# Gate and up products of the second feed-forward part by Strassen's seven half-size products

## The chip, the cores and the metric

The kernel runs on one core of one Trainium2 chip. The number that counts is the device time of one execution in microseconds (us). A core has five engines with a queue of instructions each: PE multiplies matrices, DVE (VectorE) and ACT (ScalarE) work element by element, POOL (GpSimd) does so more slowly, and SP issues the transfers from memory. The engines meet at semaphores only, and each takes its own queue strictly in order.

## The reference

Two layers act on 512 tokens of width 1024. Each has a feed-forward part, a mixing block (three recurrences) and a second feed-forward part; a last norm ends it.

```
def swiglu(h, wg, wu, wd):
    return (jax.nn.silu(h @ wg) * (h @ wu)) @ wd

for i in range(DEPTH):
    h = rmsnorm(x, ffn1_norm[i])
    x = x + 0.5 * swiglu(h, ffn1_wg[i], ffn1_wu[i], ffn1_wd[i])
    x = x + mixing block of layer i
    h = rmsnorm(x, ffn2_norm[i])
    x = x + 0.5 * swiglu(h, ffn2_wg[i], ffn2_wu[i], ffn2_wd[i])
return rmsnorm(x, final_norm)
```

The change is in the second swiglu: `h @ wg` and `h @ wu` are 512 x 1024 times 1024 x 2816, and `@ wd` is 512 x 2816 times 2816 x 1024. All is float32.

## The kernel before, in words

Activations lie transposed: the 1024 features are eight tiles of 128 partitions by 512 tokens, `self.x`. To keep the accuracy of float32, every operand of a product is split into a high part (`whi`, `hh`) and a low part (`wlo`, `hl`), and each product is three matmuls: high by high (L263), high by low (L271), low by high (L272). `load_w` fetches a block of weights (`raw`, three buffers), takes the high part on ACT (L248) and the low part on DVE (L249).

`ffn` walks over 22 column tiles of 128. `gate` does for one of them 24 matmuls of 512 columns for the gate product and 24 for the up product, each pair in a bank of PSUM of its own (`mm`, three banks). DVE multiplies both by `rstd`, the reciprocal root of each token's mean square (L386, L387), ACT applies SiLU (L388), DVE multiplies (L389), and the result is split for the down product (L276, L277). So the norm's factor is applied behind the products, and products of a layer begin as soon as `x` times the gain is split (`norm`: L1180 on ACT, L1181 on DVE); the sum of squares is added up on POOL beside it (L346), and its small instructions come later, at the places in PE's order that `GATES` names.

The down products come in parts, `PARTS`: after four tiles (three in the last two parts), and one tile of the next part, eight products of 12 (or 9) matmuls of 512 columns add the part to `x` (L377). At the end of the second layer the last part goes by halves of the tokens, with 256 columns, and `finish` norms each half.

The order of each engine's queue comes from a scheduler that follows the order of the program, what the instructions need of each other, and when buffers come free. `run` calls `ffn` twice a layer, around `mix`.

Of the kernel before, what the change touches and what calls it, by code (L numbers as in the profile page):

```python
# [9 lines left out]
F32R = mybir.dt.float32r  # L10
# [7 lines left out]
L = 512  # L18
D = 1024
# [7 lines left out]
# tag: (elements of 4 bytes, buffers)  # L27
# [10 lines left out]
# parts of the products between the steps of the recurrence  # L38
# [20 lines left out]
# ---------------------------------------------------------------- layout of the small inputs  # L59
# [4 lines left out]
def constants():  # L64
    """masks and identities, from shapes alone"""
# [37 lines left out]
def layout(z):  # L103
    """every input, laid out by partition"""
# [64 lines left out]
# ---------------------------------------------------------------- the kernel  # L169
class Kernel:  # L170
# [63 lines left out]
    def load_w(self, src, k, m, keep=None):  # L234
        """both parts of a [128, k, m] block of weights"""
# [21 lines left out]
    def gemm(self, ps, w, act, ks=None):  # L257
# [3 lines left out]
        for k in ks or range(len(act)):  # L261
# [33 lines left out]
    def row_sums(self, parts, bank):  # L295
        """per token, the sum over partitions"""
# [8 lines left out]
    def token_rstd(self, b, n, tag):  # L305
        """(b / n + eps) ** -0.5 of each token"""
# [6 lines left out]
    def row_diag(self, b, n, tags):  # L313
        """(b / n + eps) ** -0.5 of each token, in two parts, on diagonals"""
# [13 lines left out]
    def row_wide(self, dg, out, bank):  # L328
        """the diagonal on all partitions"""
# [21 lines left out]
    def norm(self, gain, gates):  # L351
        """x * gain in two parts, and the broadcast rstd of each token"""
# [14 lines left out]
    # ------------------------------------------------------------ SwiGLU  # L367
    def ffn(self, gain, f, i, end=False):
# [27 lines left out]
        for n, (k0, nk) in enumerate(PARTS):  # L396
            # the next part's first tile goes before this part's products
# [7 lines left out]
            if end and first is None:  # L405
                # the last products by halves of the tokens, to begin the last norm early
# [16 lines left out]
    # ------------------------------------------------------------ the mixing block  # L423
    def mix(self, i):
# [16 lines left out]
        def proj(j, post):  # L441
            """projection j in steps, and what is done with it"""
# [27 lines left out]
        def add():  # L470
            # the norm of the SSD part comes last
# [53 lines left out]
        def stream():  # L525
# [5 lines left out]
            # capital: all of it, else a part  # L531
# [18 lines left out]
        def weave(main, filler, ratio, pin=True):  # L550
            """main, and the filler's steps between its own"""
# [19 lines left out]
        # the recurrence first; the other products are held back to go beside it  # L571
# [47 lines left out]
    # ------------------------------------------------------------ RWKV-7  # L619
# [11 lines left out]
    def shifted(self, ps, j, out):  # L631
        """token shift of projection tile j"""
# [8 lines left out]
    def sigmoid(self, t):  # L641
        """from tanh(x / 2)"""
        self.nc.gpsimd.tensor_scalar(out=t, in0=t, scalar1=0.5, scalar2=0.5, op0=MUL, op1=ADD)

    def rwkv_l(self, ps):
        """decay, in-context rate and gate"""
# [6 lines left out]
        # [hi, lo] beside both parts of the weights, in one product where the rows allow it  # L653
# [24 lines left out]
        for ct in range(2):  # L678
# [14 lines left out]
            # cumulative sum inside chunks of 32  # L693
# [71 lines left out]
    def to_tok(self, src, out):  # L765
        """src(ct) [128 (head, d), L] -> out [128 tok, 4 token tiles, 4 heads, 64]"""
# [10 lines left out]
    def rwkv_core(self):  # L777
        """everything that the state does not enter; J = (token tile, head), in two halves of the tokens"""
# [16 lines left out]
        # masked products inside chunks of 32  # L795
        for q, M in ((0, MB), (1, MK)):
            for h in range(2):
# [11 lines left out]
                if q == 0:  # L809
                    # minus the transposed inverse of I + A, by doubling the size of its blocks  # L810
# [58 lines left out]
    def rwkv_ends(self):  # L869
        """what a chunk does to the state, S -> P S + G, the state before each chunk, and the output"""  # L870
# [14 lines left out]
        def PG(h):  # L885
            # the state before the first chunk is zero, the one after the last is not asked for
# [32 lines left out]
        def YQ(h):  # L919
            """how the state is read, and what the chunk gives by itself"""  # L920
# [75 lines left out]
        # capital: all of it, else one step  # L996
# [26 lines left out]
        # softplus(x) = max(x, 0) + log1p(exp(-|x|)), log1p(e) = 2 atanh(e / (2 + e))  # L1023
# [30 lines left out]
    def ssd_conv(self, ps, g, j):  # L1054
        """causal convolution and SiLU of x (two tiles), B and C of a group"""
# [17 lines left out]
    def ssd_chunk(self, g, c, banks=("ms",) * 4):  # L1073
# [18 lines left out]
        # decay between the tokens of a chunk, transposed  # L1092
# [84 lines left out]
    def split_scaled(self, x, scale):  # L1177
        """both parts of x * scale"""
# [21 lines left out]
    def s5_tables(self, i):  # L1200
        """what the recurrence does over chunks of 8 tokens; partitions: (part, state) or (token, channel)"""
# [25 lines left out]
        # angles in [-pi, pi]  # L1227
# [30 lines left out]
        # (a - 1) / A  # L1258
# [302 lines left out]
```

## Time and profile before

| | us |
|---|---|
| median of 3 runs | 2126.94 (2123.63 to 2130.07) |
| the profiled execution: its span | 2125.2 |
| PE busy | 2061.9 (97%) |
| DVE busy | 1261.3 (59%) |
| ACT busy | 733.2 (34%) |
| second feed-forward part, layer 0: from the norm's start to its end | 682 to 1050 |
| the same, layer 1 | 1729 to 2110 |

The span runs from the first to the last instruction of the profiled execution. "Busy" of PE counts the time in which a matmul is in its pipeline, so starts of successive matmuls tell its rate better than durations: a row's duration is longer than the distance to the next one. A note in brackets, as [1.52 <-DVE wlo L249], is the idle time before the instruction and what ended it. Names such as `mm<-hh,whi` are the tile written and the tiles read.

### The profile page before, as it was taken

The numbers are of one execution on the slowest core, as the hardware profiler recorded it, in microseconds if no ns is written. First come the engines' busy times: TensorE is split into PE (matmuls) and PEld (weight loads), VectorE is DVE, ScalarE is ACT, GpSimd is POOL, SyncE is SP. The second block draws the span as 40 slices with busy tenths as digits, with TensorE's granted clock in tenths as the row PEclk, the third lists the DMA queues.
The fourth block names the chain that finished last, engine by engine and source line by source line (L and its number), as shares of the span: only waits on it lengthen the run. The fifth ranks groups of instructions, "written<-read, shape, count | busy, mean of one in ns | idle before, by whom it ended". The sixth has DMA issues, their size and how long they took to land.

```text
span 2125.2 us, 34484 instructions
## 1 busy us (share of the span) xinstructions
PE 2061.9 (97%) x13872; PEld 1651.5 (78%) x13872; DVE 1261.3 (59%) x2072; ACT 733.2 (34%) x1068; POOL 415.5 (20%) x739
## 2 busy tenths in 40 slices
PE   7999999898999999999999999999999989999997
PEld 5888887686777788888778888877777678888886
DVE  6555554786579644444666455558856785444445
ACT  4222222543453322222432222235334433222223
POOL 2142224413221100000104302272322110000002
PEclk9999999999999999999999999999999999999998
DMA  4322332421102333223333332334111222333232
GB/s 155 105 81 84 109 100 81 148 85 41 52 26 77 111 109 96 89 80 92 107 90 110 105 90 80 92 111 139 60 53 34 59 95 70 105 109 101 83 99 70
DMA packets 87135, 190.24 MB, mean 90 GB/s; under 512 B 18752, under 2 KB 34112, under 8 KB 86976
## 3 DMA queue, kind: packets, MB, share of 16 engines
q1 hardware_dynamic: 82240, 186.85, 29.3%
q8 instruction: 110, 1.80, 0.4%
q10 hardware_dynamic: 4736, 1.18, 0.3%
q14 instruction: 49, 0.40, 0.1%
HBM read 179.48 MB, written 7.34 MB: 88 GB/s over the span
## 4 chain that ended last, share of the span: by engine, by line
PE 89%; DVE 7%; issue 2%; ACT 1%; DMA 0%; POOL 0%; SPq 0%; POOLq 0%; DVEq 0%; ACTq 0%
PE mm L263 27%; PE mm L272 26%; PE mm L271 26%; DVE wlo L249 2%; DVE hl L1181 1%; PE mr L823 1%; PE ms L1134 1%; PE mr L899 0%; PE ms L1098 0%; PE mc L952 0%; PE mr L861 0%; DVE x L377 0%; PE ms L1432 0%; PE mr L895 0%; PE ms L1433 0%
## 5 line engine op out<-in xcount | busy, mean ns | idle before, releaser
L263 PE MATMUL mm<-hh,whi 128*128 128x512 f32 x1872 | 756.3, 404 | 11.1 <-ACT whi L248 5.8
L272 PE MATMUL mm<-hh,wlo 128*128 128x512 f32 x1872 | 741.3, 396 | 15.5 <-DVE wlo L249 15.4
L271 PE MATMUL mm<-hl,whi 128*128 128x512 f32 x1872 | 738.5, 395 | 3.6 <-DVE hl L1181 2.1
L248 ACT ACTIVATE whi<-raw 128x1024 fp32r<-128x1024 f32 (+3 forms) x453 | 365.6, 808 | 996.0 <-PE mm L271 823.0
L249 DVE TENSOR_TENSOR wlo<-raw,whi 128x1024 fp32r<-128x1024 f32 (+3 forms) x453 | 430.9, 951 | 47.9 <-ACT whi L248 47.5
L272 PEld LDWEIGHTS mm<-hh,wlo 128*128 128x128 f32 x1872 | 355.4, 190 | 100.1 <-DVE wlo L249 19.9
L263 PEld LDWEIGHTS mm<-hh,whi 128*128 128x128 f32 x1872 | 356.1, 190 | 93.1 <-issue 6.8
L271 PEld LDWEIGHTS mm<-hl,whi 128*128 128x128 f32 x1872 | 356.0, 190 | 80.7 <-DVE hl L1181 4.7
L346 POOL TENSOR_TENSOR y<-up 128x512 f32<-128x512 f32 (+1 forms) x8 | 10.3, 1292 | 755.7 <-ACT up L343 755.7
L377 DVE SCALAR_TENSOR_TENSOR x<-mm,x 128x512 f32<-128x512 f32 (+1 forms) x124 | 83.3, 673 | 108.8 <-PE mm L272 108.6
L387 DVE TENSOR_TENSOR y<-mm,rstd 128x512 f32<-128x512 f32 x44 | 30.4, 692 | 138.0 <-PE mm L272 138.0
L387 DVE TENSOR_TENSOR w<-mm,rstd 128x512 f32<-128x512 f32 x44 | 30.4, 690 | 132.8 <-PE mm L272 132.8
L272 PE MATMUL mm<-bk,wlo 128*128 128x512 f32 x248 | 98.0, 395 | 4.0 <-DVE wlo L249 3.8
L263 PE MATMUL mm<-bk,whi 128*128 128x512 f32 x248 | 97.6, 394 | 1.1 <-DVE x L377 1.1
L271 PE MATMUL mm<-bk,whi 128*128 128x512 f32 x248 | 96.9, 391 | 0.0
L386 DVE TENSOR_TENSOR kk<-mm,rstd 128x512 f32<-128x512 f32 x44 | 30.4, 691 | 110.5 <-PE mm L272 110.5
L272 PE MATMUL mm<-qr,wlo 128*128 128x512 f32 x240 | 94.4, 394 | 0.0
L271 PE MATMUL mm<-qr,whi 128*128 128x512 f32 x240 | 94.2, 393 | 0.0
L263 PE MATMUL mm<-qr,whi 128*128 128x512 f32 x240 | 93.3, 393 | 0.0
L386 DVE TENSOR_TENSOR sq<-mm,rstd 128x512 f32<-128x512 f32 x44 | 30.3, 688 | 77.4 <-PE mm L272 77.4
L263 PE MATMUL mm<-bh,whi 128*128 128x512 f32 x192 | 75.8, 395 | 0.0
L272 PE MATMUL mm<-bh,wlo 128*128 128x512 f32 x192 | 75.1, 391 | 0.0
(542 smaller groups left out, 2610.8 us busy)
## 6 DMA issues: line engine op xcount, KB each, us to landing
raw<-in_ffn_wu SPq DMA_DIRECT2D x88, 512.0 KB, 3.5
raw<-in_ffn_wg SPq DMA_DIRECT2D x87, 512.0 KB, 3.5
raw<-in_ffn_wd SPq DMA_DIRECT2D x128, 256.0 KB, 2.7
raw<-in_w_in SPq DMA_DIRECT2D x42, 512.0 KB, 3.5
raw<-in_ffn_wd SPq DMA_DIRECT2D x64, 192.0 KB, 2.3
raw<-in_w_out SPq DMA_DIRECT2D x32, 128.0 KB, 2.1
raw<-in_w_out SPq DMA_DIRECT2D x16, 256.0 KB, 2.6
xd<-x SPq DMA_DIRECT2D x12, 256.0 KB, 2.5
```

Of the source, the lines that this page charges most:

```text
L248: nc.scalar.activation(out=hi[:, q], in_=raw[:, q], func=AF.Copy)
L249: sub = nc.vector.tensor_tensor(out=lo[:, q], in0=raw[:, q], in1=hi[:, q].bitcast(F32), op=SUB)
L263: first = nc.tensor.matmul(out=ps, lhsT=hi[:, k], rhs=ah, start=(k == 0), stop=False)
L271: nc.tensor.matmul(out=ps, lhsT=hi[:, k], rhs=al, start=False, stop=False)
L272: mm = nc.tensor.matmul(out=ps, lhsT=lo[:, k], rhs=ah, start=False, stop=(k == last))
L346: nc.gpsimd.tensor_tensor(out=a2, in0=acc, in1=sq, op=ADD)
L377: nc.vector.scalar_tensor_tensor(out=x, in0=pd, scalar=0.5, in1=x, op0=MUL, op1=ADD)
L386: nc.vector.tensor_tensor(out=s, in0=pg, in1=rstd, op=MUL)
L387: nc.vector.tensor_tensor(out=u, in0=pu, in1=rstd, op=MUL)
L823: nc.tensor.matmul(out=b[s, j], lhsT=lh[s, j], rhs=rh[s, j], start=True, stop=True)
L1134: nc.tensor.matmul(out=b[64 * hp:64 * hp + 64, 0, j], lhsT=X[:, 2 * j + hp], rhs=ED[:, 2 * j + hp], start=True, stop=True)
L1181: self.nc.vector.scalar_tensor_tensor(out=lo, in0=x, scalar=scale, in1=hi.bitcast(F32), op0=MUL, op1=SUB)
```

## The change

The second feed-forward part of both layers is done by a new function, `ffn_halves`. The gate and up products of two column tiles at a time (256 columns of the weight) are cut into halves in each of the three directions: the 1024 features into two interleaved halves of four tiles, the 256 weight columns into two of 128, the 512 tokens into two of 256. The eight products of quarters that this needs are replaced by seven, in Winograd's form of Strassen's algorithm. The operands are B11, B21, B22 (quarters of the activations) and T1 to T4 (their sums and differences), and on the weights' side the quarters and S0 to S3. Each of the seven takes four tiles of features, three matmuls each: 84 matmuls of 256 columns for a pair of tiles.

The sums and differences are made on DVE: those of the activations once per layer, in `norm_halves` (L398 to L400), those of the weights in each call of `halves` (L461 to L474). Some products are added up in one bank (T2 and T3 on top of B11 in `r1`; B22 on top of T1 in `r3`), and ACT copies a bank out between two of them (`snap`, L455, L468, L471, L480). DVE makes the four quarters of the result (L458, L479, L482, L488). `rstd`, SiLU and the low parts now take 1024 columns at a time (L506 to L510).

Down products are in `PAIRED` parts of 4, 4, 4, 4, 4 and 2 tiles and use the two `ms` banks. `GATES_HALVES` is where the norm's small products stand. Everything else is unchanged in meaning; comments were taken out, so that line numbers differ.

```diff
+PAIRED = ((0, 4), (4, 4), (8, 4), (12, 4), (16, 4), (20, 2))
+HALVES = "b0", "b1", "b2", "b4", "b5", "b6", "x", "x"
+GATES_HALVES = 28, 44
...
+    def norm_halves(self, gain, gates):
...
+            full = h[:, odd].rearrange("p c t -> p (c t)")
+            nc.scalar.activation(out=full, in_=self.x[k], func=AF.Copy, scale=self.gn(gain, k))
+            if not odd:
+                b = self.t("hh", [128, 2, H], F32R)
+                self.split(h[:, 0, 0], b[:, 0], b[:, 1])
+                ops.append({"B11": (b[:, 0], b[:, 1])})
+                return
+            hi, lo = self.t("hh", [128, 2, H], F32R), self.t("hl", [128, 2, H], F32R)
+            self.split(h[:, 1], hi, lo)
+            ops[q]["B21"], ops[q]["B22"] = (hi[:, 0], lo[:, 0]), (hi[:, 1], lo[:, 1])
+            flat = h.rearrange("p o c t -> p (o c) t")
+            nc.vector.tensor_tensor(out=T[:, 0:2], in0=flat[:, 1::2], in1=flat[:, 0:2], op=SUB)
+            nc.vector.tensor_tensor(out=T[:, 2], in0=h[:, 1, 1], in1=T[:, 0], op=SUB)
+            nc.vector.tensor_tensor(out=T[:, 3], in0=T[:, 2], in1=h[:, 1, 0], op=SUB)
+            hi, lo = (self.t(HALVES[2 * q + j], [128, 4, H], F32R) for j in range(2))
+            self.split(T, hi, lo)
+            for j, n in enumerate(("T1", "T3", "T2", "T4")):
+                ops[q][n] = hi[:, j], lo[:, j]
...
+    def product(self, ps, w, ops, name, first=True, last=True):
+        hi, lo = w
+        for q, op in enumerate(ops):
+            ah, al = op[name]
+            mm = nc.tensor.matmul(out=ps, lhsT=hi(q), rhs=ah, start=first and q == 0, ...)
...
+            nc.tensor.matmul(out=ps, lhsT=hi(q), rhs=al, ...)
+            mm = nc.tensor.matmul(out=ps, lhsT=lo(q), rhs=ah, ...)
+    def halves(self, w, ops, out, n):
...
+        self.split(raw[0], *w1)
+        r1 = bank()
+        self.product(r1, [at(a, 0) for a in w1], ops, "B11", last=False)
+        nc.scalar.activation(out=snap[:, 0], in_=r1, func=AF.Copy)
+        r2 = bank()
+        self.product(r2, [at(a, 1) for a in w1], ops, "B21")
+        V.tensor_tensor(out=out[:, 0, 0:H], in0=r2, in1=snap[:, 0], op=ADD)
+        V.tensor_tensor(out=S[:, 0], in0=quarter(1, 0), in1=quarter(1, 1), op=ADD)
+        V.tensor_tensor(out=S[:, 1], in0=S[:, 0], in1=quarter(0, 0), op=SUB)
+        self.split(f(S[:, 0:2]), *w2)
+        self.product(r1, [at(a, 1) for a in w2], ops, "T2", first=False, last=False)
+        nc.scalar.activation(out=snap[:, 1], in_=r1, func=AF.Copy)
+        r3 = bank()
+        self.product(r3, [at(a, 0) for a in w2], ops, "T1", last=False)
+        nc.scalar.activation(out=snap[:, 2], in_=r3, func=AF.Copy)
+        V.tensor_tensor(out=S[:, 2], in0=quarter(0, 0), in1=quarter(1, 0), op=SUB)
+        V.tensor_tensor(out=S[:, 3], in0=quarter(0, 1), in1=S[:, 1], op=SUB)
+        self.split(f(S[:, 2:4]), *w3)
+        self.product(r1, [at(a, 0) for a in w3], ops, "T3", first=False)
+        V.tensor_tensor(out=out[:, 1, H:L], in0=r1, in1=snap[:, 2], op=ADD)
+        nc.scalar.activation(out=snap[:, 3], in_=r1, func=AF.Copy)
+        self.product(r3, [at(a, 1) for a in w3], ops, "B22", first=False)
+        V.tensor_tensor(out=out[:, 0, H:L], in0=r3, in1=snap[:, 1], op=ADD)
+        self.split(quarter(1, 1), *w4)
+        r4 = bank()
+        self.product(r4, [...], ops, "T4")
+        V.tensor_tensor(out=out[:, 1, 0:H], in0=snap[:, 3], in1=r4, op=SUB)
...
+    def ffn_halves(self, gain, f, i, end=False):
...
+        def gate(p):
+            s, u = (self.t("p", [128, 2, L]) for _ in range(2))
+            self.halves(wg[2 * p:2 * p + 2], ops, s, 0)
+            nc.vector.tensor_tensor(out=s, in0=s, in1=wide, op=MUL)
+            nc.scalar.activation(out=s, in_=s, func=AF.Silu)
+            self.halves(wu[2 * p:2 * p + 2], ops, u, 1)
+            nc.vector.tensor_tensor(out=u, in0=u, in1=wide, op=MUL)
+            nc.vector.tensor_tensor(out=u, in0=u, in1=s, op=MUL)
+            g = slots[p % 3]
+            self.split(u, g[:, :, 0:L], g[:, :, L:2 * L])
...
-                for _ in self.ffn("n2", "ffn2", i, i == depth - 1):
-                    pass
+                self.ffn_halves("n2", "ffn2", i, i == depth - 1)
```

How the change moves the queues is shown at three places of layer 0. The first is PE's queue in the second feed-forward part. Before, one product of 512 columns ends and the next begins in another bank (`mm_6845`, `mm_6884`); the words in brackets are what an instruction waits for.

```order
L263 MATMUL mm_6845<-hh_6702,whi_6848 128x512
L271 MATMUL mm_6845<-hl_6703,whi_6848 128x512
L272 MATMUL mm_6845<-hh_6702,wlo_6849 128x512
L263 MATMUL mm_6884<-hh_6648,whi_6887 128x512 [waits DVE_49,Activation_49]
L271 MATMUL mm_6884<-hl_6649,whi_6887 128x512
L272 MATMUL mm_6884<-hh_6648,wlo_6888 128x512
```

Now, in an up call (one of `halves` for wu; `hh` with `whi_7827` is B11, `b0` to `b6` with `whi_7862` is T2):

```order
L423 MATMUL mm_7831<-hh_6723,whi_7827 128x256
L428 MATMUL mm_7831<-hh_6723,whi_7827 128x256
L429 MATMUL mm_7831<-hh_6723,wlo_7828 128x256
L423 MATMUL mm_7831<-b0_6663,whi_7862 128x256 [waits Activation_49]
L428 MATMUL mm_7831<-b1_6664,whi_7862 128x256
L429 MATMUL mm_7831<-b0_6663,wlo_7863 128x256 [waits DVE_49]
```

T2 is put right behind B11 and adds into the same bank, `mm_7831`. Its first matmul waits for ACT, which reads that bank (the copy of L455) and makes `whi_7862`. In gate calls B21 stands between the two.

The second place is DVE's queue at the end of the norm. Before, the last low parts of the norm (`hl`) alternate with adds of the output product (L464) and low parts of weights (`wlo`), and then the small instructions of the norm's factor begin (L309):

```order
L1181 SCALAR_TENSOR_TENSOR hl_6679<-yf_6269,gain_70,hh_6678 128x512
L464 TENSOR_TENSOR b3_6300<-mm_6626,b3_6300 128x512
L249 TENSOR_TENSOR wlo_6748<-raw_6745,whi_6747 128x1024
L464 TENSOR_TENSOR b3_6300<-mm_6640,b3_6300 128x512
L1181 SCALAR_TENSOR_TENSOR hl_6687<-yf_6269,gain_70,hh_6686 128x512
L249 TENSOR_TENSOR wlo_6779<-raw_6776,whi_6778 128x1024
L1181 SCALAR_TENSOR_TENSOR hl_6695<-b3_6300,gain_70,hh_6694 128x512
L249 TENSOR_TENSOR wlo_6818<-raw_6815,whi_6817 128x1024
L1181 SCALAR_TENSOR_TENSOR hl_6703<-b3_6300,gain_70,hh_6702 128x512
L309 TENSOR_SCALAR rrmrv_6716<-mr_6711 128x4
```

Now (`ES`, `QG` hold the scaled activations and their differences, later also the sums of weights; `b6_6714` and `x_6739` are low parts of T1 to T4, `wlo_6823` that of S0 and S1):

```order
L281 TENSOR_TENSOR b6_6714<-QG_6696,b5_6713 128x1024
L281 TENSOR_TENSOR hh_6723<-ES_6721,hh_6723 128x256
L400 TENSOR_TENSOR ES_6721<-ES_6721 128x256
L281 TENSOR_TENSOR hl_6732<-ES_6721,hh_6731 128x512
L461 TENSOR_TENSOR QG_6819<-raw_6784 128x512
L473 TENSOR_TENSOR QG_6819<-raw_6782,raw_6784 128x512
L281 TENSOR_TENSOR x_6739<-ES_6721,x_6738 128x1024
L462 TENSOR_TENSOR QG_6819<-QG_6819,raw_6782 128x512
L458 TENSOR_TENSOR p_6780<-mm_6805,bon_6786 128x256
L474 TENSOR_TENSOR QG_6819<-raw_6782,QG_6819 128x512
L281 TENSOR_TENSOR wlo_6823<-QG_6819,whi_6822 128x1024
L281 TENSOR_TENSOR wlo_6856<-QG_6819,whi_6855 128x1024
```

The differences, their low parts of 1024 columns and the sums of weights L461 to L474 stand ahead of the first low part that T2 and T1 need, `wlo_6823`; the factor's small instructions have moved behind these.

The third place is ACT's queue where the factor `rstd` of the same norm is copied out. Before:

```order
L248 ACTIVATE whi_6887<-raw_6885 128x1024
L335 ACTIVATE rstd_6710<-mr_6737 128x512
L388 ACT_TABLE_LOAD
L388 ACTIVATE sq_6806<-sq_6806 128x512
L248 ACTIVATE whi_6918<-raw_6916 128x1024
L276 ACTIVATE bk_6741<-w_6807 128x512
L388 ACTIVATE kk_6876<-kk_6876 128x512
```

Now (`bon_` copies belong to gate calls, `g_` copies to up calls; `p_6780` is the gate's result of the first pair):

```order
L339 ACTIVATE rstd_6746<-mr_6773 128x512
L280 ACTIVATE whi_7107<-QG_7071 128x1024
L468 ACTIVATE bon_7038<-mm_7043 128x256
L507 ACT_TABLE_LOAD
L507 ACTIVATE p_6780<-p_6780 128x1024
L480 ACTIVATE g_6910<-mm_6915 128x256
L280 ACTIVATE whi_7138<-raw_7036 128x512
L280 ACTIVATE whi_7163<-raw_7158 128x1024
L471 ACTIVATE bon_7038<-mm_7091 128x256
```

The table load and the first SiLU stand ahead of the copy of L480, `g_6910`, with which the bank `r1` of the first up call comes free; before, there was no copy of a bank behind them but the products' low and high parts.

## Rows read from the trace of the kernel before

**Rows 1.** The page of the profile: the span, PE's share, the chain by engine and line
```profile
span 2125.2 us, 34484 instructions
PE 2061.9 (97%) x13872; PEld 1651.5 (78%) x13872; DVE 1261.3 (59%) x2072; ACT 733.2 (34%) x1068; POOL 415.5 (20%) x739
...
PE 89%; DVE 7%; issue 2%; ACT 1%; DMA 0%; POOL 0%; SPq 0%; POOLq 0%; DVEq 0%; ACTq 0%
PE mm L263 27%; PE mm L272 26%; PE mm L271 26%; DVE wlo L249 2%; DVE hl L1181 1%; PE mr L823 1%; PE ms L1134 1%; PE mr L899 0%; PE ms L1098 0%; PE mc L952 0%; PE mr L861 0%; DVE x L377 0%; PE ms L1432 0%; PE mr L895 0%; PE ms L1433 0%
```

**Rows 2.** Table by stretches: busy us and count of each engine, PEclk, DMA share
```profile
core 0: us, PE busy (x) PEld busy (x) DVE busy (x) ACT busy (x) POOL busy (x), PEclk, DMA share, GB/s
697.00:1050.00 353.00, 352.97 (x1548) 290.09 (x1549) 170.30 (x236) 100.49 (x136) 3.34 (x2) 1.00 0.32 93
```

**Rows 3.** Timeline of PE: start us, us, engine, line, operation, tiles, shape, count
```profile
2084.05 0.39 PE L272 MATMUL mm<-hh,wlo 128*128 128x512 f32 x1
2088.16 0.39 PE L272 MATMUL mm<-hh,wlo 128*128 128x512 f32 x1
...
2105.26 0.28 PE L271 MATMUL mm<-bk,b 128*128 128x256 f32 x1
2108.20 0.28 PE L272 MATMUL mm<-qr,b 128*128 128x256 f32 x1
```

**Rows 4.** Timeline of DVE, end of the output product and norm, layer 0
```profile
681.45 0.41 DVE L249 TENSOR_TENSOR wlo<-raw,whi 128x256 fp32r<-128x256 f32 x1
681.78 0.68 DVE L476 TENSOR_TENSOR b<-up,b 128x512 f32<-128x512 f32 x1
682.38 0.68 DVE L464 TENSOR_TENSOR x<-mm,x 128x512 f32<-128x512 f32 x1
...
701.60 1.22 DVE L249 TENSOR_TENSOR wlo<-raw,whi 128x1024 fp32r<-128x1024 f32 x1
702.73 0.74 DVE L1181 SCALAR_TENSOR_TENSOR hl<-b,gain,hh 128x512 fp32r<-128x512 f32 x1
```

**Rows 5.** Timeline of PE and DVE at the end; groups of ACT lines by form
```profile
2110.36 0.28 PE L272 MATMUL mm<-qr,g 128*128 128x256 f32 x1
...
2110.68 0.42 DVE L377 SCALAR_TENSOR_TENSOR b<-mm,b 128x256 f32<-128x256 f32 x1 [0.36 <-PE mm L272]
...
L833 ACT ACTIVATE x<-mr 128x256 f32<-128x256 f32 x16 | 6.0, 375 | 21.7 <-PE mr L823 21.6
...
L248 ACT ACTIVATE whi<-raw 128x1024 fp32r<-128x1024 f32 x34 | 36.1, 1062 | 97.0 <-PE mm L271 69.4 <-issue 27.6
```

**Rows 6.** Timeline of DVE and POOL, norm of layer 0's second part
```profile
685.90 1.82 DVE L1181 SCALAR_TENSOR_TENSOR hl<-x,gain,hh 128x512 fp32r<-128x512 f32 x1
688.57 0.74 DVE L1181 SCALAR_TENSOR_TENSOR hl<-x,gain,hh 128x512 fp32r<-128x512 f32 x1
695.14 1.83 DVE L249 TENSOR_TENSOR wlo<-raw,whi 128x1024 fp32r<-128x1024 f32 x1
...
685.86 1.30 POOL L346 TENSOR_TENSOR y<-up 128x512 f32<-128x512 f32 x1 [11.96 <-ACT up L343]
699.08 2.05 POOL L346 TENSOR_TENSOR y<-w,up 128x512 f32<-128x512 f32 x1 [0.79 <-ACT up L343]
```

**Rows 7.** Timeline of PE in the same norm, with the idle time before
```profile
692.97 0.51 PE L272 MATMUL mm<-hh,wlo 128*128 128x512 f32 x1 [1.52 <-DVE wlo L249]
...
697.03 0.50 PE L272 MATMUL mm<-hh,wlo 128*128 128x512 f32 x1 [2.38 <-DVE wlo L249]
```

**Rows 8.** Timeline of ACT and DVE, ends of the first two pairs
```profile
711.49 1.28 ACT L388 ACT_TABLE_LOAD   x1
...
720.25 0.69 DVE L387 TENSOR_TENSOR y<-mm,rstd 128x512 f32<-128x512 f32 x1 [2.75 <-PE mm L272]
...
742.22 0.69 DVE L387 TENSOR_TENSOR y<-mm,rstd 128x512 f32<-128x512 f32 x1 [3.36 <-PE mm L272]
```

**Rows 9.** Timeline of POOL, the last norm
```profile
2111.80 3.46 POOL L1540 TENSOR_TENSOR hl<-hl,hh 128x256 f32<-128x256 f32 x5
```

More of the change, by code (lines that the diff above doesn't have):

```diff
@@ new lines, in product @@
+    def product(self, ps, w, ops, name, first=True, last=True):
+        nc = self.nc
+        hi, lo = w
+        for q, op in enumerate(ops):
+            ah, al = op[name]
+            mm = nc.tensor.matmul(out=ps, lhsT=hi(q), rhs=ah, start=first and q == 0, stop=False, skip_group_check=True)
+            gate = self.gates.pop(0) if self.gates else None
+            if gate is not None:
+                self.tc.add_manual_dep(gate[0], self.gemmed, BEHIND, reason="issue order")
+                self.behind(mm, gate[1])
+            nc.tensor.matmul(out=ps, lhsT=hi(q), rhs=al, start=False, stop=False, skip_group_check=True)
+            mm = nc.tensor.matmul(out=ps, lhsT=lo(q), rhs=ah, start=False, stop=last and q == len(ops) - 1,
+                                  skip_group_check=True)
+            self.gemmed = mm.ins.name
@@ new lines, in ffn_halves, with down @@
+    def ffn_halves(self, gain, f, i, end=False):
+        nc = self.nc
+        wg, wu, wd = (self.a[f"{f}_{w}"][i] for w in ("wg", "wu", "wd"))
+        ops, rstd = self.norm_halves(gain, GATES_HALVES)
+        slots = [self.t(n, [128, 2, 2 * L], F32R) for n in ("bk", "qr", "bh")]
+        wide = rstd.unsqueeze(1).to_broadcast([128, 2, L])
+        def down(gs, k0, nk, m, t=slice(0, L), w=None):
+            pd = self.bank("ms", t.stop - t.start)
+            self.gemm(pd, w or self.load_w(wd[m, :, k0:k0 + nk], nk, 128), [(gh[:, t], gl[:, t]) for gh, gl in gs])
+            x = self.x[m][:, t]
+            nc.vector.scalar_tensor_tensor(out=x, in0=pd, scalar=0.5, in1=x, op0=MUL, op1=ADD)
+        def gate(p):
[8 more added lines that the diff above has]
+            self.split(u, g[:, :, 0:L], g[:, :, L:2 * L])
+            gs.extend((g[:, j, 0:L], g[:, j, L:2 * L]) for j in range(2))
+        gs, left = [], []
+        for n, (k0, nk) in enumerate(PAIRED):
+            first = k0 + nk if n + 1 < len(PAIRED) else None
+            while len(gs) < k0 + nk:
+                gate(len(gs) // 2)
+            for d in left:
+                down(*d)
+            if end and first is None:
+                ws = [self.load_w(wd[m, :, k0:k0 + nk], nk, 128, q)
+                      for m, q in enumerate(("b0", "b1", "b2", "b4", "b5", "b6", "bon", "g"))]
+                for h in range(2):
+                    t = slice(256 * h, 256 * h + 256)
+                    for m in range(KD):
+                        down(gs[k0:], k0, nk, m, t, ws[m])
+                    self.finish(h)
+                return
+            if first is not None:
+                gate(first // 2)
+            m1 = KD - LEFT if end and n == len(PAIRED) - 2 else KD
+            left = [(gs[k0:k0 + nk], k0, nk, m) for m in range(m1, KD)]
+            for m in range(m1):
+                down(gs[k0:k0 + nk], k0, nk, m)
```

44 lines of the change are left out of this document (added).

## Prediction

> **What bounds the kernel now.** I read the page first, then the gate stretches, then the starts of single instructions. On the page PE is busy 97% of 2125.2 us, and the chain that ended last is 89% PE and 7% DVE, its first line the products of L263 [rows 1]. In the stretch of the second feed-forward part of layer 0 (697 to 1050 us) PE is busy 352.97 of 353.00 us at a granted clock of 1.00, that is at the 2.4 GHz level, DVE 170.30 us and ACT 100.49 us [rows 2]. So the gate and up products are limited by the number of columns that PE streams and by nothing else; DVE has half of its time free. The place where this doesn't hold is the norm ahead of it, where PE waited 1.52 and 2.38 us for a wlo of DVE [rows 7]. So I ask of the change: how many columns go, whether DVE and ACT still keep ahead, and what the norm's start does.
>
> **Products.** A 512-column matmul starts every 0.2283 us (2084.05 to 2088.16, 18 intervals), a 256-column one every 0.1176 us (2105.26 to 2108.20, 25 intervals) [rows 3]. Two column tiles of a gate or up product are 48 matmuls of 512 columns before, 10.96 us, and one call of `halves` is 7 x 4 x 3 = 84 of 256 columns, 9.87 us. That is -1.09 us a call, and over 2 layers x 11 pairs x 2 = 44 calls -48 us, if PE never waits. (A half-width matmul costs 0.515 of a whole one, so 7/8 becomes 0.90.)
>
> **DVE in a call.** From occupancies, start to start: 1.13 us for 1024 columns, 0.60 for 512, 0.33 for 256 [rows 4]. A call has splits of 3 x 1.13 + 0.60 = 3.99, four sums of weights 4 x 0.60 = 2.40, four outputs 4 x 0.33 = 1.32, the factor rstd 1.13, and half of a u*s and of a low part of g, 1.13: 9.97 us beside 9.87 of PE. Before, it was two splits of 1024 and four to six passes of 512, 4.7 us beside 10.96. So in a run of gates alone DVE is now the longer engine by a hair. In the steady cycle (two pairs, then eight down products of twelve 512-column matmuls, 21.9 us of PE and 9.6 us of DVE) it is 49.5 us of DVE beside 61.4 of PE: it fits on average.
>
> **Waits inside a call.** Two calls in a cycle are u-calls where T2 stands right behind B11 on PE and adds into the same bank, which ACT must first have copied (the order rows of PE). The copy of a 256-column bank takes 0.377 us, and a reader begins 0.32 us after the start of the last matmul [rows 5]. With 0.1 for the hand-over that is 0.32 + 0.38 + 0.1 - 0.12 = 0.7 us of waiting, twice a cycle. Behind that I find about 0.85 us a cycle more, where the copy of T1 stands behind a Silu of 1024 (two of 512 before; about 1.06 us, as a whi of that size takes [rows 5]) and where w4's low part is late. Ends for these waits: 0 (all hidden) and the point where DVE sets the pace, below. Taken: a cycle of 4 calls gains 4.35 - 1.4 - 0.85 = 2.1 us; four cycles a layer, -8.4 us.
>
> **The norm and the first pairs.** Before, DVE is busy without a gap from the first add of the output product, 682.38, to the last low part of the norm, 702.73 + 0.66 [rows 4]: 15.1 us of work by the occupancies (the low parts of the norm at 0.74 less 0.08 of overlap) in 21.0 us, so 5.9 us are lost. Seven adds of POOL lie in that stretch, 1.30 to 2.05 us each, and a low part that takes 0.74 us alone took 1.82 us beside one, a wlo 1.83 us instead of 1.22 [rows 6]. Now T1 and T2 need all four quarters of the activations' differences and the weights' S0 and S1. Up to the first w2 low part DVE has 43 to 44 instructions in its order from the first add: 6 of 1024, 20 of 512, 18 of 256, or 6.8 + 12.0 + 5.9 = 24.7 us. With the 5.9 lost that ends at 713.0; with the hand-overs from ACT between (a whi of 1.06 us [rows 5] must lie between the sums and the split) I take 715.5. PE can have done only B11 and B21 and four matmuls of the 168 of the pair by then; the other 140 take 16.5 us, so the first pair ends about 732.4, where before its last output was read at 720.25 [rows 8]: +12.2. Ends: 713.0 gives +9.7; POOL losses of twice the size +18.
>
> Pair 2 costs 19.74 us of PE. DVE there has 20 us of calls and also the rest of rstd, thirteen small instructions at 0.2 and two of 512, 3.8 us. And on ACT the fourth copy of the first u-call, which frees the bank that B21 of the next call wants, stands behind rstd, a table load of 1.28 us [rows 8] and the first Silu (the order rows of ACT): about 2.6 us of PE. Sum: 19.74 + 2.6 + 0.7 + 1.9 = 24.9, end 757.3 against 742.22 [rows 8], +15.1. Pair 3 goes at DVE's 20 us and 0.9 of waits, 778.2 against 764.2 (742.22 + 21.92): +14.0. With the cycles a layer comes to 14.0 - 8.4 = +5.6 us.
>
> **The ends of both parts.** The last part of the down products has two tiles, where before it had three; PE has 8 x 6 x 0.2283 = 11.0 us there instead of 16.4 to hide the next norm's start, or at the very end 16 x 6 x 0.1176 = 11.3 instead of 16.9. Between layers DVE has some 20 us there for adds, splits and low parts: 0 to +4.6, I take +2. At the end the pieces follow each other at 0.70 us of PE, and the last additions by POOL take 0.69 each (five in 3.46) [rows 9]: 0 to +2.8, I take +1.5.
>
> **Nothing** I put on the transfers: a call loads the same 1 MB, the DMA share is 0.32 [rows 2], and PE's faster calls need at most a tenth more. The small re-orderings elsewhere in layer 1 I put at 0, +-2.
>
> Sum: 2 x 5.6 + 2 + 1.5 = +14.7 us on a span of 2125.2. The runs shown have a median of 2126.94, 1.7 us above that span, so I forecast 2126.9 + 14.7 = 2141.6, rounded to 2141 us.
>
> The Trainium skill ("SBUF — State Buffer", section "Who interferes with whom") says that a DVE instruction with two inputs in SBUF and a GpSimd instruction that reads SBUF exclude each other, and that the other one blocks for the whole time. The stretched rows agree with it, though a stretched low part lost only 0.6 to 1.1 us and not a whole 1.3 each time [rows 6]. If every one of seven adds cost DVE its whole 1.3 us, because nearly all of the norm's instructions now have two such inputs, that is 9.1 in place of 5.9: +3.2 us a layer, 2148 us.
>
> **Rivals.**
> (B) The saving shows. Of the waits in a cycle only 0.85 of my 2.25 us are there, the norm's start costs only the lower end, +9, pair 2 nothing, pair 3 gives 2 back, and a cycle gains 3.5: 9 - 2 - 14 = -7 a layer; with +3 for the ends -11 us: 2116 us. For it: DVE's average in the cycle is 81%, and three buffers of weights lie between. Against it: T2 behind B11 on one bank is fixed in the order.
> (C) DVE, not PE, sets the pace in every run of gates, since its queue also holds the outputs that wait for PE, and each such wait delays a split behind it. At 11.5 us a call the cycles lose 2 us each instead of gaining: 2 x (14 + 8) = +44: 2171 us. For it: 9.97 beside 9.87. Against it: the down products give DVE 12 us of slack a cycle. It decides once a call takes longer than the 10.96 us of before.
> (D) A wash: start +10, four cycles at -2.75, ends +3: (10 - 11) x 2 + 3 = +1: 2128 us. It takes a norm near the lower end and cycles between mine and B's.
> That the products are not reduced I exclude: the order has 84 matmuls of 256 columns a call.
>
> **How the numbers follow.** Forecast 0.47, B 0.20, C 0.17, D 0.16. A measurement here can tell 0.3% from no change, 6.4 us. Faster: B, 0.20. Same: most of D and a little of the forecast's lower side, 0.17. Slower 0.63. The range from 2112 to 2168 takes the forecast with its bounds, D, the upper part of B and the lower half of C; the likeliest case's own range is 2132 to 2155.
>
> **What would show it.** Right: the first pair of layer 0 ends 10 to 14 us later after the first output add than before; PE idles before T2 of u-calls by about 0.7 us with ACT as the releaser; a cycle of 2 pairs and 8 downs takes 63 to 64 us instead of 65.8; DVE near 100% in the first three pairs and 75 to 85% later. Wrong: cycles of 62 us or less (B), or PE idle behind DVE splits in each call (C); a matmul interval over 0.12 us in the gates; a granted clock below 1.00 there, which no row of before shows in this stretch.

## The result and the profile after

The changed kernel takes 2154.69 us (median of 4 runs, 2154.11 to 2157.62) against 2128.51 us before (4 runs): ratio 1.0132, 95% interval [1.0111, 1.0154]. It is slower, as forecast, but by about twice as much: the medians lie 26.2 us apart, and its profiled execution spans 2155.8 us, 30.6 us more than that of before, where the sum had 14.7.

The page of the changed kernel:

```profile
span 2155.8 us, 38261 instructions
PE 2047.8 (95%) x15432; PEld 1705.8 (79%) x15432; DVE 1511.6 (70%) x2456; ACT 874.1 (41%) x1312; POOL 417.2 (19%) x739
...
PEclk9999999999999799999999999999999989999998
```

PE is busy 14 us less than in [rows 1] and DVE 250 us more. The PEclk line has a 7 in the slice from 700 to 754 us, where the second feed-forward part of layer 0 begins. The table by stretches shows it closer, first this start, then the four cycles of two pairs and eight down products:

```profile
core 0: us, PE busy (x) PEld busy (x) DVE busy (x) ACT busy (x) POOL busy (x), PEclk, DMA share, GB/s
704.00:724.00 20.00, 11.47 (x41) 9.37 (x42) 18.30 (x26) 9.62 (x15) 2.99 (x2) 0.50 0.13 38
789.57:1045.45 255.88, 251.17 (x1730) 231.59 (x1729) 205.30 (x290) 119.01 (x177) 3.25 (x8) 1.00 0.34 99
```

For 20 us PE ran at the 1.2 GHz level (0.50 in the PEclk column). What it did before and during that, from PE's timeline (last column: idle time before, and its releaser):

```profile
704.58 0.58 PE L429 MATMUL mm<-hh,wlo 128*128 128x256 f32 x1 [4.84 <-DVE wlo L281]
...
712.72 1.10 PE L423 MATMUL mm<-hh,whi 128*128 128x256 f32 x2 [3.29 <-ACT hh L280]
...
719.09 0.58 PE L423 MATMUL mm<-b,whi 128*128 128x256 f32 x1 [3.23 <-ACT whi L280]
...
721.16 0.41 PE L429 MATMUL mm<-b,wlo 128*128 128x256 f32 x1
721.37 0.41 PE L423 MATMUL mm<-b,whi 128*128 128x256 f32 x1
...
740.25 0.28 PE L429 MATMUL mm<-hh,wlo 128*128 128x256 f32 x1
...
746.70 0.39 PE L423 MATMUL mm<-hh,whi 128*128 128x256 f32 x1 [2.14 <-ACT g L480]
```

Where before there were waits of 1.52 and 2.38 us [rows 7], there are now 4.84, 3.29 and 3.23 us, and successive matmuls of 256 columns then start 0.21 us apart (721.16, 721.37), not 0.118 as in [rows 3]. 740.25 is the 168th of the seven-product matmuls, the last of pair 1. The half clock lasts from 703.9 us, within the wait of 4.84 us, to 724.4 us, and comes again for 3.4 us at 748.3, behind the wait of 2.14 us; layer 1 has the same, 20.5 and 3.4 us. Before, the start of layer 0's part had none and that of layer 1's 3.4 us, from 1744.4, at the end of a wait of 2.44 us.

The outputs that end pairs 2 and 3 of layer 0, its first and fourth cycle, and pair 3 and the fourth cycle of layer 1, from DVE's timeline:

```profile
766.95 0.42 DVE L488 TENSOR_TENSOR p<-g,mm 128x256 f32<-128x256 f32 x1
...
785.56 0.42 DVE L488 TENSOR_TENSOR p<-g,mm 128x256 f32<-128x256 f32 x1 [0.92 <-PE mm L429]
...
849.49 0.42 DVE L488 TENSOR_TENSOR p<-g,mm 128x256 f32<-128x256 f32 x1 [0.92 <-PE mm L429]
...
1041.44 0.42 DVE L488 TENSOR_TENSOR p<-g,mm 128x256 f32<-128x256 f32 x1 [0.92 <-PE mm L429]
...
1844.62 0.42 DVE L488 TENSOR_TENSOR p<-g,mm 128x256 f32<-128x256 f32 x1 [0.92 <-PE mm L429]
...
2101.71 0.42 DVE L488 TENSOR_TENSOR p<-g,mm 128x256 f32<-128x256 f32 x1 [0.92 <-PE mm L429]
```

All are read against the mixing block's rstd, which lies just ahead (664.88 us before, 668.25 after; in layer 1 1712.2 and 1728.1). In the kernel before, this rstd and the output that ends the same fourth cycle are:

```profile
664.88 0.60 ACT L335 ACTIVATE rstd<-ms 128x512 f32<-128x512 f32 x1
...
1005.29 0.69 DVE L387 TENSOR_TENSOR y<-mm,rstd 128x512 f32<-128x512 f32 x1 [4.34 <-PE mm L272]
```

Pair 3 ends 117.3 us behind the rstd in layer 0 and 116.5 in layer 1; before, by the second pair's 742.22 [rows 8] plus 21.97 for two more tiles, 99.3 and 101.0. So the start loses 18.0 and 15.5 us. A cycle takes 63.97 us (layer 0: 1041.44 less 785.56, by four) and 64.27 (layer 1: 2101.71 less 1844.62), against 65.77 before (1005.29 less 742.22, by four).

In the cycles nearly all of PE's longer waits are at one place. The sum of its waits in the four cycles of layer 0, and one of them in the timeline (T2 of an up call):

```profile
PE mm L423 <- ACT g L455: 3.8, 8, 0.5
PE mm L423 <- DVE p L458: 0.5, 1, 0.5
```

```profile
819.69 0.28 PE L429 MATMUL mm<-hh,wlo 128*128 128x256 f32 x1
820.44 0.39 PE L423 MATMUL mm<-b,whi 128*128 128x256 f32 x1 [0.47 <-ACT g L455]
820.67 0.28 PE L428 MATMUL mm<-b,whi 128*128 128x256 f32 x1
```

Eight times in four cycles T2 waits for the copy of B11; an idle time of 0.47 us costs 0.75 from start to start, and the next matmul comes 0.23 us later. That is 0.74 us a time above the bare intervals, 5.9 us of the 10.5 us by which PE's starts in these four cycles exceed them. The other 4.6 us are one wait of 0.49 us (the second line of the sum) and many delays of 0.1 to 0.3 us, too short for that view. One of them is at the third matmul of T4, which needs the low part of w4; PE's two starts and DVE's low part:

```profile
826.59 0.28 PE L428 MATMUL mm<-b,whi 128*128 128x256 f32 x1
826.90 0.38 PE L429 MATMUL mm<-b,wlo 128*128 128x256 f32 x1
...
826.16 0.68 DVE L281 TENSOR_TENSOR wlo<-raw,whi 128x512 fp32r<-128x512 f32 x1
```

### The profile page after: what moved, and what is told of

It reads as the page before. It is cut to its first block, busy times and chain, and to the rows that moved or that the text cites. A ratio compares the mean times of both kernels' runs of the same rounds, so it can differ in the third digit from the quotient of the medians.

```text
span 2155.8 us, 38261 instructions
## 1 busy us (share of the span) xinstructions
PE 2047.8 (95%) x15432; PEld 1705.8 (79%) x15432; DVE 1511.6 (70%) x2456; ACT 874.1 (41%) x1312; POOL 417.2 (19%) x739
## 5 line engine op out<-in xcount | busy, mean ns | idle before, releaser
L252 ACT ACTIVATE whi<-raw 128x512 fp32r<-128x512 f32 (+3 forms) x365 | 273.1, 749 | 658.8 <-PE mm L275 492.3
L267 PE MATMUL mm<-hh,whi 128*128 128x512 f32 x1168 | 480.9, 412 | 9.0 <-ACT whi L252 6.0
L276 PE MATMUL mm<-hh,wlo 128*128 128x512 f32 x1168 | 466.1, 399 | 13.4 <-DVE wlo L253 13.4
L275 PE MATMUL mm<-hl,whi 128*128 128x512 f32 x1168 | 465.8, 399 | 2.7 <-DVE hl L281 1.4
L253 DVE TENSOR_TENSOR wlo<-raw,whi 128x512 fp32r<-128x512 f32 (+3 forms) x365 | 327.3, 897 | 48.3 <-ACT whi L252 47.0
L423 PE MATMUL mm<-b,whi 128*128 128x256 f32 x528 | 153.1, 290 | 17.8 <-ACT g L455 8.5
L423 PE MATMUL mm<-hh,whi 128*128 128x256 f32 x528 | 152.6, 291 | 12.7 <-ACT hh L280 6.6
L429 PE MATMUL mm<-hh,wlo 128*128 128x256 f32 x528 | 148.7, 285 | 9.7 <-DVE wlo L281 9.7
L429 PE MATMUL mm<-b,wlo 128*128 128x256 f32 x528 | 150.9, 286 | 0.4
L428 PE MATMUL mm<-b,whi 128*128 128x256 f32 x528 | 150.4, 285 | 0.0
L423 PEld LDWEIGHTS mm<-b,whi 128*128 128x128 f32 x528 | 101.7, 193 | 23.8 <-ACT g L455 12.2
L429 PEld LDWEIGHTS mm<-hh,wlo 128*128 128x128 f32 x528 | 101.0, 193 | 10.4 <-DVE wlo L281 10.1
L428 PEld LDWEIGHTS mm<-b,whi 128*128 128x128 f32 x528 | 101.5, 192 | 0.1
L350 POOL TENSOR_TENSOR y<-up 128x512 f32<-128x512 f32 (+1 forms) x8 | 10.2, 1269 | 464.1 <-ACT up L347 464.1
```

Source lines behind the costliest of these rows:

```text
L252: nc.scalar.activation(out=hi[:, q], in_=raw[:, q], func=AF.Copy)
L253: sub = nc.vector.tensor_tensor(out=lo[:, q], in0=raw[:, q], in1=hi[:, q].bitcast(F32), op=SUB)
L267: first = nc.tensor.matmul(out=ps, lhsT=hi[:, k], rhs=ah, start=(k == 0), stop=False)
L275: nc.tensor.matmul(out=ps, lhsT=hi[:, k], rhs=al, start=False, stop=False)
L276: mm = nc.tensor.matmul(out=ps, lhsT=lo[:, k], rhs=ah, start=False, stop=(k == last))
L350: nc.gpsimd.tensor_tensor(out=a2, in0=acc, in1=sq, op=ADD)
```

## The experiments

The kernels with e, with f and with g in front ran on one chip for each letter, beside the kernel before (medians there 2125.75, 2127.47 and 2126.39 us, and 2128.51 beside the changed kernel). The changed kernel was not run again, so a difference to it of under some 3 us says nothing. "u*s" is DVE's product of pair 3's up result with SiLU (L510), in us behind the mixing rstd, for layers 0 and 1; the cycle is the mean of the whole cycles of layer 0. Both are read from one profiled execution of each kernel.

| kernel | median us | ratio to before [95%] | u*s of pair 3 | cycle |
|---|---|---|---|---|
| changed | 2154.69 | 1.0132 [1.0111, 1.0154] | 121.3, 120.5 | 63.97 |
| e_warm | 2145.69 | 1.0094 [1.0076, 1.0113] | 117.5, 117.4 | 64.2 |
| e_plain | 2140.57 | 1.0069 [1.0053, 1.0086] | 114.2, 114.6 | 64.1 |
| e_b21 | 2160.08 | 1.0161 [1.0142, 1.0180] | 123.8, 123.5 | 64.2 |
| e_ends | 2166.29 | 1.0190 [1.0172, 1.0208] | 121.0, 119.4 | 64.0 |
| f_two | 2113.11 | 0.9927 [0.9912, 0.9941] | 102.4, 100.9 | 63.8 |
| f_bank | 2125.06 | 0.9985 [0.9972, 0.9997] | 116.0, 116.5 | 61.4 |
| f_ends3 | 2150.63 | 1.0106 [1.0087, 1.0125] | 121.3, 121.3 | 64.1 |
| g_bank | 2126.00 | 0.9996 [0.9985, 1.0007] | 116.0, 116.0 | 61.6 |
| g_one | 2110.67 | 0.9923 [0.9909, 0.9937] | 110.6, 111.0 | 61.3 |
| f_best | 2089.42 | 0.9816 [0.9799, 0.9833] | 102.1, 102.0 | 60.8 |

**e_warm: matmuls without use in PE's idle time.**

```diff
+        self.idle = {("B11", 0, 2): 41, ("B11", 3, 0): 34, ("T2", 0, 0): 30}
...
+        for j in range(n):
+            mm = self.nc.tensor.matmul(out=ps, lhsT=self.ones, rhs=ops[0]["B11"][0], start=True, stop=True, ...)
+            self.behind(mm, last)
```

> In the first gate call of both layers 41, 34 and 30 matmuls without use (256 columns, into a bank that nobody reads) stand at the three places where PE waited 4.84, 3.29 and 3.23 us. Theory 1: the granted clock stays at 1.00 through the norm, the T products at 719 to 725 us go at 0.118 instead of 0.215 us each and pair 1 ends 2 to 2.5 us earlier; 1 to 3 us a layer, 2149 to 2153 us. Rival (the half clock is hidden behind DVE's queue): the clock is at 1.00 and pair 2 and 3 end when they did, 2153 to 2157 us.

The stretch that answers to 704:724, in the table by stretches:

```profile
701.00:721.00 20.00, 16.22 (x122) 14.79 (x121) 18.24 (x26) 10.70 (x16) 2.81 (x2) 1.00 0.13 42
```

The clock stays at 1.00 (in layer 1 all but 3.4 us at 1764.9), u*s of pair 3 comes 3.9 and 3.1 us earlier, and the time falls by 9.0 us, more than expected; by the ratios it is 8, and the two intervals just meet. DVE has the same work (18.24 and 18.30 us in 20). Of the 8.9 us between the two profiled executions 7.4 lie in the two parts. T2 begins 50.8 us behind the rstd in the changed kernel and 50.9 in e_warm, in both layers, so the waits ahead of it are only covered, not gone. By the end of pair 1 e_warm is 1.7 and 0.9 us ahead, less than expected. The rest comes in pair 2, where the second stretch at half clock is gone and the wait of 2.14 us has shrunk:

```profile
740.15 0.39 PE L436 MATMUL mm<-hh,whi 128*128 128x256 f32 x1 [0.96 <-ACT g L496]
```

So keeping the clock up is worth 3 to 4 us at each start, of which 1 to 2 us are the slow matmuls themselves; how much of the rest is owed to the changed order of the queues was not separated.

**e_plain and f_two: the first pair, or the first two, by ordinary products.**

```diff
-        ops, rstd = self.norm_halves(gain, GATES_HALVES)
+        ops, rstd, act, differences = self.norm_halves(gain, GATES[2])
...
+            for j in range(2):
+                for src, out in ((wg, s), (wu, u)):
+                    ps = self.bank("mm")
+                    self.gemm(ps, self.load_w(src[2 * p + j], KD, 128), act)
+                    nc.vector.tensor_tensor(out=out[:, j], in0=ps, in1=rstd, op=MUL)
+                if j == 0:
+                    differences()
...
+                self.behind(first, self.diag)
```

The last line, which keeps the differences behind the norm's factor on DVE, and the second plain pair (`p < 2`, differences with `p == 1`) are in f_two alone.

> The first pair of tiles of both layers is done by ordinary 512-column products, the norm is the one of the kernel before, and the differences T1 to T4 are made behind it, beside the first pair's products. Theory 1 (the loss sits in the start: T1 and T2 wait for all differences, and PE's idle time halves the clock there): the third pair, which ended 18.1 us (layer 0) and 15.5 us (layer 1) late, ends at most 4 us late in each layer, no half clock after the norm, and the time is 22 to 30 us below the changed kernel's 2154.7, 2125 to 2133 us. Theory 2 (DVE sets the pace of all gates): the later pairs lose again what the first gains, DVE near 100% to the third pair and beyond, 2146 us or more.

> The first two pairs of tiles of both layers are done by ordinary 512-column products; the norm is the one of the kernel before; DVE's first differences stand behind the last instruction of the norm's factor. With one plain pair (e_plain) DVE still made differences ahead of low parts that PE waited for. Theory 1 (the loss is the start, through the order on DVE and the half clock that PE's idle time brings): the third pair's u*s comes 100 to 103 us after the mixing norm's rstd (kernel before about 100.3, changed kernel 121.4 and 120.5, e_plain 114.2 and 114.5), no half clock there, 35 to 42 us off, 2112 to 2120 us. Theory 2 (DVE's pace): it comes at 108 us or later and the cycles grow, 2130 us or more.

e_plain fell short: 14 us instead of 22 to 30. Written behind the first products, the differences still went ahead of the norm's factor in DVE's queue, and PE waited for it:

```profile
723.96 0.77 PE L336 MATMUL mr<-tm,ones 128*128 128x512 f32 x1 [5.54 <-DVE tm L327]
```

With that order forced and two pairs as cover, f_two comes out in its band, 41.6 us below the changed kernel. Rstd of the mixing block and u*s of pair 3 in f_two, and the same of the changed kernel:

```profile
664.42 0.60 ACT L339 ACTIVATE rstd<-ms 128x512 f32<-128x512 f32 x1
...
766.80 1.22 DVE L515 TENSOR_TENSOR p<-p 128x1024 f32<-128x1024 f32 x1
```

```profile
668.25 0.60 ACT L339 ACTIVATE rstd<-ms 128x512 f32<-128x512 f32 x1
...
789.57 1.22 DVE L510 TENSOR_TENSOR p<-p 128x1024 f32<-128x1024 f32 x1
```

102.4 us against 121.3, and 100.5 before (99.3 to the output and 1.2 on DVE): the start's loss is all but gone, though only one pair of three has seven products. Some half clock stays, against expectation, 6.8 us at 694.9 in layer 0 and 3.4 us in layer 1, at waits of up to 1.66 us. The cycles are as slow as in the changed kernel (63.8). This kernel is faster than the kernel before.

**e_b21, f_bank, g_bank: the waits in the cycles.**

```diff
-        self.product(r1, [at(a, 1) for a in w2], ops, "T2", first=False, last=False)
+        self.product(r1, [at(a, 1) for a in w2], ops, "T2", first=False, last=False, after=b21)
```

```diff
+        other = "mr" if self.normed else "mm"
...
-        r2 = bank()
+        r2 = bank(other)
...
-        r4 = bank()
+        r4 = bank(other)
```

e_b21 has the first edit, g_bank the second, f_bank both (`normed` is set behind the first pair).

> In every call T2's first matmul is kept behind B21's last one, so that the copy of B11 has a product's time (1.4 us) to be done. Theory (the wait for that copy, 0.75 us in each of the 20 up calls where T2 followed B11, is a loss of its own): no idle time of PE before T2 with ACT as releaser, a cycle of 62.7 instead of 64.1 us, 10 to 15 us off the time, 2140 to 2145 us. Rival (the wait moves to a split or another copy): cycles of 63.5 us or more, 2149 us or more.

> T2 stands behind B21, as in e_b21, and from the second pair on B21 and T4 go into the two banks mr instead of the three mm. In e_b21 PE's wait for the copy of B11 went and a wait of B21 for the earlier call's last copies came, so that nothing was won. Theory (five banks let both go): no idle time of PE in the cycles, 62.3 to 63 us instead of 64.0, and no wait of 2 us in pair 2: 12 to 18 us off, 2137 to 2143 us. Rival (DVE's or ACT's queue then sets the same time): 63.7 us or more a cycle, 2150 us or more.

> Of f_bank only the banks: from the second pair on B21 and T4 go into the two banks mr, and T2 is not held behind B21. If the banks alone did it (T2 followed B11 because B21's bank was not free, not because of its place in the program): cycles of 61.3 to 61.6 us as in f_bank, 2123 to 2130 us. If the hold is needed: PE idle again before T2 by 0.47 us with ACT as the releaser, cycles of 63 us or more, 2138 us or more.

In e_b21 the wait only moved: from T2 to B21 of the up call that follows. One of the new waits, and their sum over four cycles:

```profile
883.36 0.38 PE L423 MATMUL mm<-hh,whi 128*128 128x256 f32 x1 [0.75 <-ACT bon L482]
```

```profile
PE mm L423 <- ACT bon L482: 3.8, 8, 0.7
PE mm L423 <- DVE p L490: 2.9, 4, 1.2
```

The start lost 2.4 and 3.0 us more as well. The kernel is 5 us slower than the changed one, with intervals that overlap; the gain of 10 to 15 us is not there, and the rival was right. Two more banks end it. The four cycles of layer 0 in f_bank, and all that PE waits in them:

```profile
780.15:1025.72 245.57, 244.92 (x1724) 229.36 (x1723) 203.50 (x288) 118.08 (x176) 3.25 (x8) 1.00 0.33 103
```

```profile
PE mr L423 <- DVE p L491: 0.6, 1, 0.6
```

245.57 us by four is 61.4, which is PE's bare sum (39.5 + 21.9). The time falls by 29.6 us, more than the 12 to 18 expected: by the traces 2.6 us in each cycle of layer 0 and 3.0 in layer 1, and 5.4 and 4.0 us up to pair 3. g_bank shows that the banks alone do it. DVE has the same work as in the changed kernel (203.50 and 205.30 us), so its rate did not set the pace. What the banks change is PE's order: in f_bank T4 begins at 813.26, DVE makes w4's low part at 813.29, and PE does the twelve matmuls of B22 before it needs that part at 814.91, where the changed kernel stood still at 826.90.

**e_ends and f_ends3: the parts of the down products.**

```diff
-PAIRED = ((0, 4), (4, 4), (8, 4), (12, 4), (16, 4), (20, 2))
+PAIRED = ((0, 4), (4, 4), (8, 4), (12, 4), (16, 2), (18, 4))
```

f_ends3 has `(16, 3), (19, 3)` there, and `gate(len(gs) // 2)` in place of `gate(first // 2)`.

> The down products go in parts of 4, 4, 4, 4, 2 and 4 tiles, so that the last part has four tiles and not two. Theory (a last part of two tiles is too short on PE to hide the next norm's work and the pieces of the last norm): the crossing to layer 1 costs 0 to 1 us instead of 2.7, the end 0 to 2 instead of 5.2, less 1 to 2 us for the part of two tiles in the middle: 2148 to 2152 us. Rival (the end's 5.2 us come from elsewhere): 2154 us or more.

> Down products in parts of 4, 4, 4, 4, 3 and 3 tiles, as in the kernel before; unlike e_ends, a pair of gates always stands between the last pair's low parts and the products that need them. Theory (the short last part costs at the crossing and at the end): 4 to 7 us off, 2148 to 2151 us. Rival (those microseconds do not come from the part's length): within 1.5 us of the changed kernel, 2153 us or more.

e_ends is a miss, 11.6 us slower: with these parts the last pair stands right ahead of the products that need it. PE's first such product, from its timeline:

```profile
1057.90 1.22 PE L267 MATMUL ms<-qr,whi 128*128 128x512 f32 x2 [3.00 <-ACT qr L280]
```

f_ends3 avoids that and gains 4.1 us, but its interval overlaps that of the changed kernel. By the traces layer 0, from mixing rstd to the next layer's first rstd, takes 423.2 us and not 425.9 (before: 412.4), while the end of layer 1 (last u*s to the end of the span) stays at 49.8 us, 50.1 in the changed kernel. So the crossing's 2.7 us came from the short part, as far as one trace of each shows; the end's 5.2 did not.

**f_best and g_one: what is left when the causes are taken away together.**

> Two plain pairs, five banks with T2 behind B21, and parts of 4, 4, 4, 4, 3 and 3 tiles together. If the three losses are separate: about 40 + 10 + 5 us off the changed kernel, 2096 to 2106 us, 1% or more below the kernel before. If they share one cause (DVE or ACT full): 2115 us or more.

> As f_best, but only the first pair by ordinary products, so that two more calls have seven products, and the differences must be done on DVE within one pair. If DVE gets them done in time: 2.2 us a layer better, 2084 to 2087 us. If T1 and T2 of the second pair wait for them (by the sum of DVE's work behind the factor, some 18 us, about 5 us late): 2092 to 2098 us.

f_best has f_two's start, f_bank's banks and f_ends3's parts. The first two lines of its page:

```profile
span 2088.3 us, 37649 instructions
PE 2022.0 (97%) x15168; PEld 1682.6 (81%) x15168; DVE 1462.7 (70%) x2384; ACT 850.9 (41%) x1264; POOL 420.7 (20%) x739
```

It is 65.3 us below the changed kernel and 1.84% faster than the kernel before (interval 1.67 to 2.01%), below the expected 2096 to 2106, where f_bank's edit had been put at 10 us. The three alone brought 41.6, 29.6 and 4.1 us, 75.3 in all; 9.3 us of f_bank's lie up to pair 3, where f_best is no earlier than f_two, and 75.3 less 9.3 is near the 65.3. g_one differs by one plain pair and is 21 us slower, where 3 to 9 were expected for the bad case. PE's wait at T1 and T2 of its second pair:

```profile
731.59 0.58 PE L411 MATMUL mm<-b,whi 128*128 128x256 f32 x1 [8.16 <-ACT whi L280]
```

8.16 us instead of some 5, and 10.2 us at half clock, from 726.4, within the wait: what the changed kernel has in its first pair, in another pair.

## Why the prediction was wrong

The direction was right and so were most of the places, the size was not. Term by term, forecast against trace:

| term | forecast us | measured us |
|---|---|---|
| start to pair 3, layers 0 and 1 | +14.0, +14.0 | +18.0, +15.5 |
| four cycles, layers 0 and 1 | -8.4, -8.4 | -7.2, -6.0 |
| crossing to layer 1 | +2 | +2.7 |
| end | +1.5 | +5.2 |
| outside both parts | 0 | +2.4 |
| sum | +14.7 | +30.6 |

Of the 15.9 us that are missing, the start has 5.5, the end 3.7, the cycles 3.6, the crossing 0.7, and 2.4 lie outside both parts.

**The start** is the step that failed. "The other 140 take 16.5 us" priced every matmul at 0.1176 us and put nothing else on PE. They take 19.9 us (720.35 to 740.25): 19 of them go at half clock, 1.9 us more, and among them stand the norm's own small products, with a wait of 0.23 us for the factor, 1.5 us for which the sum has no term. The walk of DVE's queue nearly held: T2 began 33.3 us after the first output add (685.75 to 719.09) and w2's low part was done 34.5 us after it, put at 33.1. But PE is idle for 12.6 of the last 19.4 us before T2, and the walk did not ask what PE's clock does then. Together pair 1 is 4.8 us late; its 168 matmuls were issued 54.5 us after the add (740.25), where 50.0 had been forecast for the read of its last output. Pairs 2 and 3 gave 0.8 us of that back. In layer 1 the term is only 1.5 us off, mainly because the kernel before is itself 1.7 us later there (101.0 against 99.3). e_warm shows what keeping the clock up gives, 3.9 and 3.1 us. "A granted clock below 1.00 there" stood among the things that would make the prediction wrong, but no rival carried it, and "no row of before shows" it is true of the rows only: the trace of before has it in layer 1, 3.4 us from 1744.4.

During that walk seven instructions of DVE are stretched beside adds of POOL; the sum puts the loss at 5.9 us. Two of the seven:

```profile
689.60 1.80 DVE L398 TENSOR_TENSOR QG<-QG 128x512 f32<-128x512 f32 x1
...
699.71 2.28 DVE L281 TENSOR_TENSOR b<-QG,b 128x1024 fp32r<-128x1024 f32 x1
```

Alone these take 0.69 and 1.22 us. Six lost 1.06 to 1.12 us, one 0.47, together 7.0: between the 5.9 of the sum and the 9.1 that the prediction gives for seven whole adds. With the sum's other numbers that is +1.1 us a layer, most of the 1.4 us by which the walk was late, and it was in the range. The Trainium skill ("SBUF — State Buffer", "Who interferes with whom") lets a DVE instruction with two inputs in SBUF and a GpSimd instruction that reads SBUF exclude each other, the second blocked while the first lasts. The trace agrees: the first of the two rows began 0.06 us behind an add of POOL (689.54, 1.31 us long) and lost most of it.

**The cycles** were nearly right, in the places too. T2's two waits cost 0.74 us each, forecast 0.7. The other 0.85 us measure 1.1 in layer 0: 0.3 at w4's low part (826.90); 0.2 at B22 (828.28), which follows the copy of T1 behind SiLU, as forecast; and 0.3 each at the first matmuls of T4 and of the next call's B11. But all of this is what three banks make of the order. With five, nearly all of the 2.6 us a cycle is gone, with the same work on DVE and ACT. The prediction took T2 behind B11 as fixed in the order, and that the number of banks is what to change was not seen.

**The copy behind the table load**, 2.6 us in pair 2, measured 2.14 [rows 8 for the load], in this order on ACT:

```profile
744.02 1.28 ACT L507 ACT_TABLE_LOAD   x1
745.32 1.06 ACT L507 ACTIVATE p<-p 128x1024 f32<-128x1024 f32 x1
746.28 0.37 ACT L480 ACTIVATE g<-mm 128x256 f32<-128x256 f32 x1
```

The matmul at 746.70 follows. f_bank has no such wait.

**The end** was under-sized by 3.7 us. Of its 5.2 us, 1.6 lie behind the last product (16.4 us to the end of the span, 14.8 before) and 2.6 in the half-token pieces, which take 3.6 us more than PE's bare time (1.0 before); 1.5 of that come with a wait of 1.33 us at 2126.85 for a bank of the down products. The last 1.0 us was not placed. The cause stays open: the part's length, which the prediction named, is not it. These pieces go round two banks (`ms`), where before they had three (`mm`); that was not tested.

Of the **rivals**, C (DVE sets the pace) is refuted by f_bank. B's mechanism, waits that are not there, is what f_bank makes; it gave -11 us with a start of +9, and f_bank, with its pair 3 still 13.2 and 12.0 us late, lands at the kernel before. D, a wash, needed a start of +10 and cycles at -2.75, and neither is there (+18.0 and +15.5, -1.8 and -1.5). The +2.4 us outside are probably not the change's: ahead of the part all these kernels have the same code, and their mixing rstd of layer 0 lies between 664.0 and 668.9 us.

## What to carry to other kernels

A seven-product scheme saves PE only what its bookkeeping leaves: count the PSUM banks that are held by a half-done sum plus the copies out of them before counting columns, since two more banks were worth 30 us here and the one other order that was tried with three (e_b21) nothing. Work that must precede the first product belongs beside products that don't need it: two pairs left as they were returned 42 us. And where a walk of the queues finds PE idle for several microseconds, as the 4.84 us here, price the matmuls behind it at the lower clock (0.21 us and not 0.118), and count what else stands between them.

## What the hardware showed that was not expected

- The granted clock fell to 0.50 (1.2 GHz) within PE's wait of 4.84 us, stayed there through the waits of 3.29 and 3.23 us, and rose 5.3 us after the last of these (719.09), 20.5 us in all; layer 1 has the same. With the waits filled it stayed at 1.00, all but 3.4 us in layer 1. Waits of 0.47 us, eight times in 256 us, left it at 1.00. The Trainium skill ("TensorE: Matmul & The Clock Gate", "A second HAM failure mode: psum-queue depth-cycling") tells of a kernel whose short idle times between groups, while it cycles through banks, made the clock swing; the cycles here also have short idle times and go round three banks, and the clock did not swing.
- A wait costs more than its idle time: 0.47 us of it is 0.75 from start to start instead of 0.12, since the 0.28 us of the matmul before, which the next one otherwise overlaps, come on top; and it is 0.23 to the next.
